# An encoder trunk of two layers: the latents' up-projection stacked on 128 rows, the first norm's rows kept in PSUM, and a newly ranked order of instructions

## The chip, the core and the metric

The kernel runs on one core of a Trainium2 chip. The metric is the device time of one execution in microseconds. Three runs of the kernel before took 1167.98, 1168.71 and 1168.90 us (median 1168.71).

## What is computed

The reference is a trunk of two post-norm layers over 512 positions of width 1024, in float32. Cut to what matters here:

```
h = layer_norm(x, ln_in_g, ln_in_b)
for l in range(2):
    a_in, b_q, b_k, b_v, c_in, d_cq, d_ckv, d_kr = split(h @ w_in[l])
    o_a = silu(layer_norm(depthwise_conv31(a_in[:256] * sigmoid(a_in[256:]))))
    o_b = attention(rope(rms_norm(b_q)), rope(rms_norm(b_k)), b_v)      # 4 heads of 64
    o_c = u * (sgu_w @ layer_norm(sv) + sgu_b)                          # u, sv = gelu(c_in)
    qd  = rms_norm(d_cq, mla_q_norm) @ mla_w_uq     # 192 latents -> 4 heads x 96
    kvd = rms_norm(d_ckv, mla_kv_norm) @ mla_w_ukv  # 128 latents -> 4 heads x 128
    o_d = attention(q, k, v from qd, kvd, rope(d_kr))                   # 4 heads of 96
    h = layer_norm(alpha * h + concat(o_a, o_b, o_c, o_d) @ w_out)
    f = conv3(h @ ffn_w_up); f = silu(f[:2816]) * f[2816:]
    h = layer_norm(alpha * h + f @ ffn_w_down)
```

## The kernel before

Positions lie in four tiles of 128. Every float32 operand of a matmul is split in a high part (rounded, made by ScalarE) and a low part (the rest, a subtraction on VectorE or GpSimd), and a product is three matmuls, high x high, high x low and low x high: `mm3` issues them. Weights come by DMA in chunks into three `raw` buffers and are split into `wh` and `wl` units on chip; the stream `h` is normalised by `ln_tile`, transposed on TensorE and split into `hh` and `hl`. PSUM has eight buffers, four called `acc` and four called `wk`.

The work of a layer is recorded as sections: the projections of the groups B (grouped-query attention), A (convolution), D (latents) and C (gating), normalisation and rotation, the up-projection of the latents (`d_up`), the attentions, the convolution's 31 steps on VectorE (`a_conv`), the output projection (`residual` with chunks O), the feed-forward part (`ffn`, chunks F) and its way down (`residual` with chunks W). In layer 0 group B comes first and A second.

The order on each engine isn't the order of recording. A planner (`Sched.place`) goes through the recorded operations with a table of costs and starts at each step the one that can begin first, by a priority: the operation's number plus the `rank` of its section. `window` and `slack` say how far ahead and how late an operation may be taken. Weight chunks have their own rule: `ahead` tells how many chunks before its use a chunk's DMA is issued, `lead` where the splitting stands. The resulting order is fixed in the program.

What the change touches: `first_rows` makes the scale and bias rows of the input's norm by transposing a column tile `incol` that is broadcast (16 transposes, four to a row of 512), each into a `wk` buffer that ScalarE copies to a unit called `row`. `LN_IN = "TTDS"` gives the four tiles' modes: T and D do the norm on VectorE (per half two instructions, `h = (h - mean) * g` and `h = h * r + b`), T at highest priority for the first half; S does it with ScalarE, VectorE and GpSimd. `rsqrt` computes r as a power on GpSimd (`vr <- ve, mhalf`). `d_evac` copies the 352 latent columns out of PSUM, `d_norm` scales them, `d_lat` transposes them (columns 0 to 127, 128 to 191 and 192 to 319) and splits them into `dTh` and `dTl`, and `d_up` multiplies: the 192 query latents are 128 rows and 64 rows, each a product of three matmuls, into the same buffer.

Of the kernel before, what the change touches and what calls it, by code (L numbers as in the profile page):

```python
# [16 lines left out]
P = 128  # L17
DM = 1024
S = 512
# [29 lines left out]
for _k in KEYS:  # L49
# [11 lines left out]
LN_IN, LN_MODES, LN_OUT = "TTDS", ["DDDD"] * 4, "DSST"  # L61
# [10 lines left out]
TUNE = {'window': 383,  # L72
         'slack': 11.0,
         'spare': 1,
         'ahead': {'A': 16, 'B': 21, 'D': 4, 'U': 18, 'V': 29, 'C': 42, 'O': 5, 'F': 6, 'W': 19},
         'lead': {'A': 19, 'B': 1, 'D': 33, 'U': 25, 'V': 3, 'C': 3, 'O': 0, 'F': 51, 'W': 13},
         'rank': {'a0': 141,
                  'a1': 91,
                  'a_norm1': -632,
                  'b1': -362,  # L80
                  'b_att0': 60,
                  'b_att1': 12,
                  'b_heads0': 234,
                  'b_heads1': -800,
                  'b_rope0': 56,
                  'b_rope1': -427,
                  'c0': -5,
                  'c1': -69,
                  'c_norm0': 147,
                  'c_norm1': -12,  # L90
                  'c_sgu0': -367,
                  'c_sgu1': -269,
                  'conv0': 481,
                  'conv1': -86,
                  'd0': 104,
                  'd_att0': -75,
                  'd_att1': -219,
                  'd_norm0': 294,
                  'd_norm1': -52,
                  'd_up0': -81,  # L100
                  'd_up1': 106,
                  'down0': -398,
                  'ffn0': -19,
                  'ffn1': 47,
                  'out0': 4,
                  'out1': -110,
                  'tables0': 1266,
                  'tables1': 123}}
# [98 lines left out]
class Op:  # L207
    __slots__ = ("eng", "cost", "tail", "lock", "calls", "deps", "succ", "nd", "prio", "ready", "allocs", "tiles", "spare",
                 "nbytes", "end", "start", "home", "sec", "after", "urgent", "table",
# [3 lines left out]
class Sched:  # L213
    ENGINES = ("SP", "PE", "DVE", "ACT", "POOL")

    def __init__(self, tc, pools):
# [3 lines left out]
        self.ops, self.group_op, self.sec, self.back, self.chunk_no = [], None, "", 0, None  # L220
# [31 lines left out]
    @contextmanager  # L252
    def chunk(self, j):

        old = self.chunk_no
        self.chunk_no = j
        yield
        self.chunk_no = old

    def record(self, eng, method, args, kw):  # L260
        op = self.group_op
        if not op:
# [4 lines left out]
            op.urgent, op.table = self.urgent, None  # L267
# [59 lines left out]
    def cost(eng, method, args, kw, outs, ins):  # L327
# [10 lines left out]
        if eng == "PE":  # L338
# [3 lines left out]
            if ins[0].shape[0] == 64 and n == 512 and psum(outs[0]) and outs[0].t.kind == "acc":  # L342
                return 115.0, 280.0, False
# [15 lines left out]
        if ALU.pow in args:  # L359
            return 290.0 + n * 165.0, 40.0, True  # L360
# [11 lines left out]
    def place(self, tune):  # L372

        extra = {}
        for op in self.ops:
            op.end, op.start, op.ready, op.spare, op.succ = 0.0, None, 0.0, 0, []
            op.nd = len(op.deps) + len(op.after)
            op.prio = -1 if op.urgent else op.index + tune["rank"].get(op.sec, 0)
            if op.chunk is not None:
                kind = KEYS[op.chunk][1]  # L380
                before = KEYS[max(0, op.chunk - tune["ahead"][kind])]
                op.home = self.first_use[before]
                if op.eng == "SP":
                    op.prio = op.chunk
                    if before in self.last_use and op.chunk >= tune["ahead"][kind]:
                        extra[op] = self.last_use[before]
                        op.nd += extra[op] not in op.deps
                else:
                    op.spare = tune["spare"]
                    op.prio = self.first_use[KEYS[max(0, op.chunk - tune["lead"][kind])]]  # L390
# [111 lines left out]
class Kern:  # L502
# [204 lines left out]
    def region(self, l, c, n, evac, single=False):  # L707
# [3 lines left out]
        for t in range(NT):  # L711
# [13 lines left out]
            evac(t, ps)  # L725
# [30 lines left out]
    def a_conv(self, l):  # L756
        s = self.s
        o = l * NPP
        for c in range(2):
# [171 lines left out]
    def b_heads(self):  # L931
        self.bq = [None] * 3
        for i in (2, 0, 1):
            ps = self.wk()
            self.transposes(ps, [y.rearrange("p h c -> p (h c)")[:, i * P:(i + 1) * P] for y in self.by])
            hi, lo = self.unit([P, S], FR, nm="bqh"), self.unit([P, S], FR, nm="bql")
            self.split(hi, lo, ps)
# [285 lines left out]
    def run(self):  # L1223
# [8 lines left out]
        for t in range(NT):  # L1232
            self.ln_tile(t, gb, LN_IN[t])
# [159 lines left out]
```

## Time and profile before

| | |
|---|---|
| median of three runs | 1168.71 us |
| the profiled execution | 1169.58 us, span 1167.8 us |
| TensorE (PE) busy | 1139.6 us, 98% |
| VectorE (DVE) busy | 778.6 us, 67% |
| ScalarE (ACT) busy | 559.7 us, 48% |
| GpSimd (POOL) busy | 162.2 us, 14% |
| mean granted clock of TensorE | 0.995 |

The span runs from the first to the last instruction. A busy share is a mean over stages that have different limits, so a stage's own windows and waits have to be read beside it. In a row of the timeline the first number is the start, the second the time from the first start to the last end of the merged instructions; in brackets stands the idle time of the engine before it, and what ended it. Matmuls overlap their neighbours, so the distance of two starts is what one costs, not its duration. The granted clock is given as a share of full speed: 1.00 is 2.4 GHz and 0.50 is 1.2 GHz.

### The profile page before, as it was taken

The numbers are of one execution on the slowest core, as the hardware profiler recorded it, in microseconds if no ns is written. First come the engines' busy times: TensorE is split into PE (matmuls) and PEld (weight loads), VectorE is DVE, ScalarE is ACT, GpSimd is POOL, SyncE is SP. The second block draws the span as 40 slices with busy tenths as digits, with TensorE's granted clock in tenths as the row PEclk, the third lists the DMA queues.
The fourth block names the chain that finished last, engine by engine and source line by source line (L and its number), as shares of the span: only waits on it lengthen the run. The fifth ranks groups of instructions, "written<-read, shape, count | busy, mean of one in ns | idle before, by whom it ended". The sixth has DMA issues, their size and how long they took to land.

```text
span 1167.8 us, 15419 instructions
## 1 busy us (share of the span) xinstructions
PE 1139.6 (98%) x5810; PEld 963.8 (83%) x5810; DVE 778.6 (67%) x1306; ACT 559.7 (48%) x1201; POOL 162.2 (14%) x205
## 2 busy tenths in 40 slices
PE   5999989999999999999999999999999999999997
PEld 4797878898888888888889888889888888888886
DVE  7798996876666755325586999967766676642425
ACT  4747897244444543223345579743544464431221
POOL 5325144100000000000022234230000000000002
PEclk9899999999999999999999999999999999999999
DMA  6520031233222522224432001222322353222311
GB/s 212 163 85 1 19 109 32 78 115 102 96 103 91 182 75 72 91 90 131 145 110 86 1 1 36 91 90 73 127 90 91 109 172 99 70 74 73 107 56 72
DMA packets 32041, 105.71 MB, mean 91 GB/s; under 512 B 3680, under 2 KB 4064, under 8 KB 31968
## 3 DMA queue, kind: packets, MB, share of 16 engines
q1 hardware_dynamic: 31968, 104.74, 27.6%
q8 instruction: 45, 0.74, 0.2%
q14 instruction: 28, 0.23, 0.1%
HBM read 102.63 MB, written 2.10 MB: 90 GB/s over the span
## 4 chain that ended last, share of the span: by engine, by line
PE 92%; ACT 4%; DVE 3%; issue 1%; DMA 1%; SPq 0%; DVEq 0%; ACTq 0%
PE acc L490 55%; PE wk L490 37%; ACT prob L490 1%; ACT pth L490 1%; DMA h<-in_x_dram 1%; DVE max L490 1%; DVE h L490 1%; DVE ptl L490 0%; ACT wh L490 0%; ACT c L490 0%; ACT dh L490 0%; ACT L490 0%; DVE mixl L490 0%; DVE aconv L490 0%; ACT do L490 0%
## 5 line engine op out<-in xcount | busy, mean ns | idle before, releaser
L490 DVE TENSOR_TENSOR wl<-raw,wh 128x512 fp32r<-128x512 f32 (+1 forms) x264 | 175.7, 700 | 94.9 <-ACT wh L490 51.7
L490 ACT ACTIVATE wh<-raw 128x512 fp32r<-128x512 f32 (+2 forms) x310 | 177.7, 614 | 55.9 <-DMA raw<-in_wst_dram 39.6
L490 PE MATMUL acc<-hh,wh 128*128 128x512 f32 (+1 forms) x544 | 191.7, 352 | 0.0
L490 PE MATMUL acc<-hh,wl 128*128 128x512 f32 (+1 forms) x544 | 191.3, 352 | 0.0
L490 PE MATMUL acc<-hl,wh 128*128 128x512 f32 (+1 forms) x544 | 191.3, 352 | 0.0
L490 PE MATMUL wk<-hh,wh 128*128 128x512 f32 x320 | 124.5, 389 | 0.0
L490 PE MATMUL wk<-hl,wh 128*128 128x512 f32 x320 | 124.5, 389 | 0.0
L490 PE MATMUL wk<-hh,wl 128*128 128x512 f32 x320 | 124.5, 389 | 0.0
L490 PEld LDWEIGHTS acc<-hl,wh 128*128 128x128 f32 x544 | 102.9, 189 | 13.7
L490 PEld LDWEIGHTS acc<-hh,wh 128*128 128x128 f32 x544 | 102.9, 189 | 13.7
L490 PEld LDWEIGHTS acc<-hh,wl 128*128 128x128 f32 x544 | 102.9, 189 | 13.7
L490 POOL TENSOR_TENSOR vr<-ve,mhalf 128x1 f32<-128x1 f32 (+2 forms) x26 | 26.6, 1021 | 593.0 <-DVE ve L490 592.9
L490 DVE SCALAR_TENSOR_TENSOR y<-acc,pp,y 128x511 f32<-128x511 f32 x96 | 71.9, 749 | 37.7 <-ACT y L490 35.8
L490 DVE TENSOR_TENSOR hl<-raw,hh 128x512 fp32r<-128x512 f32 x56 | 38.0, 690 | 83.5 <-ACT hh L490 83.5
L490 ACT ACTIVATE hh<-raw 128x512 fp32r<-128x512 f32 x56 | 35.4, 632 | 109.4 <-PE acc L490 92.0
L490 DVE SCALAR_TENSOR_TENSOR aconv<-aglu,pp,aconv 128x506 f32<-128x506 f32 (+14 forms) x120 | 86.8, 754 | 0.7
L490 PE MATMUL acc<-hl,fh 128*128 128x512 f32 x224 | 85.8, 383 | 0.0
L490 PE MATMUL acc<-hh,fh 128*128 128x512 f32 x224 | 85.7, 383 | 0.0
L490 PE MATMUL acc<-hh,fl 128*128 128x512 f32 x224 | 85.7, 382 | 0.0
L490 DVE SCALAR_TENSOR_TENSOR y<-wk,pp,y 128x511 f32<-128x511 f32 x80 | 60.0, 750 | 25.6 <-ACT y L490 23.8
L490 PE MATMUL wk<-wh,hh 128*128 128x512 f32 (+1 forms) x192 | 75.0, 391 | 0.7 <-DVE hl L490 0.7
L490 PE MATMUL wk<-wh,hl 128*128 128x512 f32 (+1 forms) x192 | 72.3, 376 | 0.0
(199 smaller groups left out, 2287.1 us busy)
## 6 DMA issues: line engine op xcount, KB each, us to landing
raw<-in_wst_dram SPq DMA_DIRECT2D x172, 512.0 KB, 3.5
row<-in_rows_dram SPq DMA_DIRECT2D x16, 256.0 KB, 4.8
raw<-in_wst_dram SPq DMA_DIRECT2D x8, 352.0 KB, 3.4
out_dram<-h SPq DMA_DIRECT2D x8, 256.0 KB, 2.0
h<-in_x_dram SPq DMA_DIRECT2D x3, 512.0 KB, 5.2
raw<-in_wst_dram SPq DMA_DIRECT2D x2, 384.0 KB, 4.0
h<-in_x_dram SPq DMA_DIRECT2D x2, 256.0 KB, 2.8
raw<-in_wst_dram SPq DMA_DIRECT2D x2, 256.0 KB, 2.8
```

What stands on the lines that cost most here:

```text
L490: f(*[a.real() if isinstance(a, View) else a for a in args], **{k: v.real() if isinstance(v, View) else v for k, v in kw.items()})
```

## The change

There are three edits.

The scale and bias rows of the first norm are transposed into `acc` buffers and stay there; VectorE reads them from PSUM, and the copies to `row` units are gone. The fourth input tile is normalised in mode D instead of S.

In the up-projection the second part of the query latents, 64 rows, is stacked: the 64 columns 128 to 191 are copied twice on evacuation (the latent unit grows from 352 to 416 columns), so that the transposed tile has the same 64 rows twice; the high part is made on all 128 rows and the lower 64 rows are then overwritten with the low part. The weight's 64 rows are laid out twice in the host's array, where zeros were before. One matmul with the weight's high part and one with its low part replace the three on 64 rows (the product low x low is computed as well).

The planner gets finer sections: a section can have parts (`with s.sub(...)`), whose rank is added to the section's, and `ahead` and `lead` can be given for a chunk kind in one layer. Three of its costs are changed, and the whole table of ranks, `ahead` and `lead` is replaced. What is recorded is otherwise the same.

```diff
-LN_IN, LN_MODES, LN_OUT = "TTDS", ["DDDD"] * 4, "DSST"
+LN_IN, LN_MODES, LN_OUT = "TTDD", ["DDDD"] * 4, "DSST"
...
-TUNE = {'window': 383,
-         'slack': 11.0,
+TUNE = {'window': 334,
+         'slack': 0.0,
...
+    @contextmanager
+    def sub(self, name):
+
+        old = self.part
+        self.part = f"{self.sec}.{name}"
+        yield
+        self.part = old
...
-                return 115.0, 280.0, False
+                return 115.0 + (200.0 if kw["start"] else 0.0) / 2 + (100.0 if kw["stop"] else 0.0) / 2, 280.0, False
...
-            return 290.0 + n * 165.0, 40.0, True
+            return 700.0 + n * 145.0, 40.0, True
...
-            op.prio = -1 if op.urgent else op.index + tune["rank"].get(op.sec, 0)
+            op.prio = -1 if op.urgent else op.index + tune["rank"].get(op.sec, 0) + tune["rank"].get(op.part, 0)
...
-                ps = self.wk()
+                ps = self.acc()
                 o = i * KD + 4 * j
                 self.transposes(ps, [self.incol[:, k:k + 1].to_broadcast([P, P]) for k in range(o, o + 4)])
-                u = self.unit([P, 512], nm="row")
-                self.s.ACT.activation(u, ps, AF.Copy)
-                res[i][j] = u
+                res[i][j] = ps
...
-            c = self.unit([P, 352], nm="dc")
+            c = self.unit([P, 416], nm="dc")
...
-            s.ACT.activation(c, ps[:, 0:352], AF.Copy)
+            s.ACT.activation(c[:, 0:192], ps[:, 0:192], AF.Copy)
+            s.ACT.activation(c[:, 192:416], ps[:, 128:352], AF.Copy)
...
-            s.ACT.activation(hi[:n], ps[:n], AF.Copy, scale=g)
-            s.DVE.scalar_tensor_tensor(lo_[:n], ps[:n], g, hi[:n].bitcast(F32), ALU.mult, ALU.subtract)
+            hi = self.unit([P, S], FR, nm="dTh")
+            g = self.pp[:, o + col:o + col + 1]
+            s.ACT.activation(hi, ps, AF.Copy, scale=g)
+            if n == P:
+                lo_, r = self.unit([P, S], FR, nm="dTl"), slice(0, P)
+            else:
+                lo_, r = hi, slice(n, P)
+            s.DVE.scalar_tensor_tensor(lo_[r], ps[r], g[r], hi[r].bitcast(F32), ALU.mult, ALU.subtract)
...
-                self.mm3(ps[:, 0:384], c1h[:64, ts], c1l[:64, ts], w1[0][:64], w1[1][:64], False, True)
+
+                s.PE.matmul(ps[:, 0:384], c1[:, ts], w1[0], start=False, stop=False)
+                s.PE.matmul(ps[:, 0:384], c1[:, ts], w1[1], start=False, stop=True)
...
-        pad = np.zeros((256, 384), uq.dtype)
-        pad[:192] = uq
-        wst.append(_ktiles(pad, 384))
+        wst.append(_ktiles(np.concatenate([uq, uq[128:]]), 384))
```

How the order moves is seen at three places. The first is VectorE at the program's start; `h_83` and `h_84` are the first and second input tiles, `mv` a tile's mean and variance, `vr` its r, and the rows are `row_...` before and `acc_...` after. Before:

```order
L490 TENSOR_SCALAR ve_119<-mv_112 128x1
L490 SCALAR_TENSOR_TENSOR h_83<-h_83,mv_112,row_121 128x512
L490 BN_STATS bst_144<-h_84 128x6 x2
L490 BN_AGGR mv_153<-bst_144 128x2
L490 SCALAR_TENSOR_TENSOR h_83<-h_83,vr_123,row_133 128x512
L490 TENSOR_SCALAR ve_163<-mv_153 128x1
L490 SCALAR_TENSOR_TENSOR h_84<-h_84,mv_153,row_121 128x512
L490 SCALAR_TENSOR_TENSOR h_83<-h_83,mv_112,row_146 128x512
L490 SCALAR_TENSOR_TENSOR h_84<-h_84,mv_153,row_146 128x512
L490 SCALAR_TENSOR_TENSOR h_83<-h_83,vr_123,row_150 128x512
```

On VectorE at the same place after the change:

```order
L610 TENSOR_SCALAR ve_119<-mv_112 128x1
L610 SCALAR_TENSOR_TENSOR h_83<-h_83,mv_112,acc_107 128x512
L610 SCALAR_TENSOR_TENSOR h_83<-h_83,vr_122,acc_114 128x512
L610 SCALAR_TENSOR_TENSOR h_83<-h_83,mv_112,acc_126 128x512
L610 BN_STATS bst_149<-h_84 128x6
L610 SCALAR_TENSOR_TENSOR h_83<-h_83,vr_122,acc_136 128x512
L610 BN_STATS bst_149<-h_84 128x6
L610 TENSOR_TENSOR hl<-wk_144,hh 128x4x128
L610 BN_AGGR mv_170<-bst_149 128x2
L610 SCALAR_TENSOR_TENSOR h_84<-h_84,mv_170,acc_126 128x512
```

All four multiplies of the first tile now stand ahead of the second tile's first multiply, with one statistics instruction between them where two and an aggregation stood.

The second place is GpSimd at the start, with the low parts `wl` of the first weight chunks and the powers `vr` of the input tiles. Before:

```order
L490 TENSOR_TENSOR wl_135<-raw_97,wh_125 128x512
L490 TENSOR_TENSOR wl_148<-raw_97,wh_137 128x512
L490 TENSOR_TENSOR vr_185<-ve_163,mhalf 128x1
L490 TENSOR_TENSOR wl_194<-raw_100,wh_155 128x512
L490 TENSOR_TENSOR wl_208<-raw_100,wh_160 128x512
L490 TENSOR_TENSOR wl_228<-raw_102,wh_172 128x512
```

On GpSimd at the same place after:

```order
L610 TENSOR_TENSOR wl_134<-raw_97,wh_124 128x512
L610 TENSOR_TENSOR wl_142<-raw_97,wh_131 128x512
L610 TENSOR_TENSOR wl_168<-raw_100,wh_161 128x512
L610 TENSOR_TENSOR wl_188<-raw_100,wh_165 128x512
L610 TENSOR_TENSOR wl_197<-raw_102,wh_184 128x512
L610 TENSOR_TENSOR vr_209<-ve_193,mhalf 128x1
L610 TENSOR_TENSOR wl_213<-raw_102,wh_190 128x512
```

The power of the second input tile moved behind three more low parts.

The third place is TensorE in the up-projection of layer 0, one position tile and the start of what follows. Before:

```order
L490 MATMUL wk_1084<-wh_375,dTh_1043 128x384
L490 MATMUL wk_1084<-wl_415,dTh_1043 128x384
L490 MATMUL wk_1084<-wh_375,dTl_1056 128x384
L490 MATMUL wk_1084<-wh_379,dTh_1047 128x384
L490 MATMUL wk_1084<-wl_425,dTh_1047 128x384
L490 MATMUL wk_1084<-wh_379,dTl_1062 128x384
L490 MATMUL wk_1096<-wh_375,dTh_1043 128x384
```

On TensorE at the same place after:

```order
L610 MATMUL wk_1167<-wh_476,dTh_1130 128x384
L610 MATMUL wk_1167<-wl_486,dTh_1130 128x384
L610 MATMUL wk_1167<-wh_476,dTl_1148 128x384
L610 MATMUL wk_1167<-wh_484,dTh_1138 128x384
L610 MATMUL wk_1167<-wl_498,dTh_1138 128x384
L610 MATMUL wk_1180<-wh_489,dTh_1150 128x512
L610 MATMUL wk_1180<-wl_507,dTh_1150 128x512
L610 MATMUL wk_1180<-wh_489,dTl_1161 128x512
```

The second part of the query latents (`dTh_1047` before, `dTh_1138` after) takes two matmuls instead of three, and the key and value part of the same position tile (the 512 columns) now follows at once instead of behind all query parts.

## Rows read from the trace of the kernel before

**Rows 1.** The page's first part: busy us, share of the span, instructions, by engine.

```profile
PE 1139.6 (98%) x5810; PEld 963.8 (83%) x5810; DVE 778.6 (67%) x1306; ACT 559.7 (48%) x1201; POOL 162.2 (14%) x205
```

**Rows 2.** Windows: stretch, length, busy us by engine (instructions), granted clock, DMA share, GB/s.

```profile
132.00:178.00 46.00, 42.08 (x264) 35.45 (x261) 44.06 (x86) 42.72 (x98) 14.18 (x12) 1.00 0.20 69
692.00:765.00 73.00, 69.54 (x428) 58.97 (x426) 63.99 (x127) 61.25 (x140) 27.38 (x27) 1.00 0.18 57
822.00:1030.00 208.00, 208.00 (x920) 172.27 (x919) 134.51 (x198) 96.61 (x158) 0.00 (x0) 1.00 0.33 107
1157.00:1168.00 11.00, 3.73 (x32) 3.52 (x30) 6.55 (x12) 0.81 (x2) 3.56 (x3) 0.82 0.25 95
```

**Rows 3.** Timeline of the start: start, us, engine, instruction, count, idle before and releaser.

```profile
5.12 3.65 PE L490 MATMUL wk<-ident,incol 128*128 128x128 f32 x16 [5.12 <-DMA incol<-in_incol_dram]
6.24 0.60 ACT L490 ACTIVATE row<-wk 128x512 f32<-128x512 f32 x1 [4.22 <-PE wk L490]
6.87 0.75 DVE L490 SCALAR_TENSOR_TENSOR h<-h,mv,row 128x512 f32<-128x512 f32 x1 [1.60 <-ACT row L490]
8.23 2.52 POOL L490 TENSOR_TENSOR wl<-raw,wh 128x512 fp32r<-128x512 f32 x2 [2.25 <-ACT wh L490]
9.03 1.29 DVE L490 BATCH_NORM_STATS2 bst<-h 128x6 f32<-128x512 f32 x2 [1.41 <-DMA h<-in_x_dram]
11.35 1.12 PE L490 MATMUL wk<-ident,h 128*128 128x128 f32 x4 [2.59 <-DVE ve L490]
11.44 0.99 POOL L490 TENSOR_TENSOR vr<-ve,mhalf 128x1 f32<-128x1 f32 x1 [0.69 <-DVE ve L490]
14.28 1.76 DVE L490 SCALAR_TENSOR_TENSOR h<-h,vr,row 128x512 f32<-128x512 f32 x1
16.09 1.12 PE L490 MATMUL wk<-ident,h 128*128 128x128 f32 x4 [3.62 <-DVE h L490]
16.86 0.78 PE L490 MATMUL wk<-wh,hh 128*128 128x512 f32 x1
17.43 0.63 PE L490 MATMUL wk<-wl,hh 128*128 128x512 f32 x1
17.86 0.63 PE L490 MATMUL wk<-wh,hl 128*128 128x512 f32 x1
29.62 1.37 PE L490 MATMUL wk<-ident,h 128*128 128x128 f32 x8 [1.67 <-issue]
```

**Rows 4.** Windows: the stretch behind the second wait.

```profile
31.60:37.00 5.40, 5.34 (x13) 4.18 (x14) 5.38 (x8) 3.63 (x7) 3.35 (x2) 0.50 0.51 174
```

**Rows 5.** The chain that ended last, in order of time: start, us, what.

```profile
31.66 17.65 PE wk L490 x68
49.31 10.88 PE acc L490 x48
```

**Rows 6.** Timeline of TensorE in the up-projections of layer 0 and of layer 1.

```profile
101.77 0.33 PE L490 MATMUL wk<-wh,dTl 128*128 128x384 f32 x1
102.03 0.44 PE L490 MATMUL wk<-wh,dTh 64*128 64x384 f32 x1
102.31 0.33 PE L490 MATMUL wk<-wl,dTh 64*128 64x384 f32 x1
102.49 0.33 PE L490 MATMUL wk<-wh,dTl 64*128 64x384 f32 x1
102.75 0.44 PE L490 MATMUL wk<-wh,dTh 128*128 128x384 f32 x1
...
690.75 0.44 PE L490 MATMUL wk<-wh,dTh 64*128 64x384 f32 x1
690.76 0.50 PE L490 MATMUL acc<-bqh,bqh 64*128 64x512 f32 x1
```

**Rows 7.** Groups of VectorE's instructions, shapes apart: busy us, mean ns, idle before.

```profile
L490 DVE SCALAR_TENSOR_TENSOR h<-h,mv,row 128x512 f32<-128x512 f32 x34 | 24.9, 773 | 1.6 <-ACT row L490 1.6
L490 DVE SCALAR_TENSOR_TENSOR h<-h,acc 128x512 f32<-128x512 f32 x31 | 21.3, 687 | 41.7 <-PE acc L490 41.7
```

More of the change, by code (lines that the diff above doesn't have):

```diff
@@ new lines @@
+         'ahead': {'A': 6,
+                   'B': 10,
+                   'D': 10,
+                   'U': 21,
+                   'V': 12,
+                   'C': 44,
+                   'O': 5,
+                   'F': 2,
+                   'W': 6,
+                   'W1': 35,
+                   'W0': 15,
+                   'C0': 42,
+                   'A1': 17,
+                   'V0': 17,
+                   'C1': 42,
+                   'F1': 6,
+                   'A0': 30,
+                   'B1': 34,
+                   'D0': 9,
+                   'F0': 5,
+                   'B0': 27,
+                   'V1': 28,
+                   'U1': 32,
+                   'U0': 40,
+                   'D1': 5},
@@ new lines @@
+         'lead': {'A': 32,
+                  'B': 14,
+                  'D': 45,
+                  'U': 73,
+                  'V': 8,
+                  'C': 0,
+                  'O': 5,
+                  'F': 37,
+                  'W': 8,
+                  'D1': 5,
+                  'A0': 11,
+                  'U1': 69,
+                  'C1': 11,
+                  'O1': 0,
+                  'D0': 22,
+                  'B1': 15,
+                  'F1': 16,
+                  'O0': 2,
+                  'U0': 84,
+                  'V1': 15,
+                  'V0': 15,
+                  'C0': 13,
+                  'B0': 3,
+                  'F0': 45,
+                  'A1': 30,
+                  'W0': 14,
+                  'W1': 6},
@@ L208 @@
     __slots__ = ("eng", "cost", "tail", "lock", "calls", "deps", "succ", "nd", "prio", "ready", "allocs", "tiles", "spare",
-                 "nbytes", "end", "start", "home", "sec", "after", "urgent", "table",
+                 "nbytes", "end", "start", "home", "sec", "after", "urgent", "table", "part",
                  "chunk", "index")
@@ L219, in __init__ @@
                         "POOL": tc.nc.gpsimd}
-        self.ops, self.group_op, self.sec, self.back, self.chunk_no = [], None, "", 0, None
+        self.ops, self.group_op, self.sec, self.part, self.back, self.chunk_no = [], None, "", "", 0, None
         self.group_wait, self.urgent = 0.0, False
@@ L377, in place @@
             op.nd = len(op.deps) + len(op.after)
-            op.prio = -1 if op.urgent else op.index + tune["rank"].get(op.sec, 0)
+            op.prio = -1 if op.urgent else op.index + tune["rank"].get(op.sec, 0) + tune["rank"].get(op.part, 0)
             if op.chunk is not None:
                 kind = KEYS[op.chunk][1]
-                before = KEYS[max(0, op.chunk - tune["ahead"][kind])]
+                layer = f"{kind}{KEYS[op.chunk][0]}"
+                ahead, lead = [tune[k].get(layer, tune[k][kind]) for k in ("ahead", "lead")]
+                before = KEYS[max(0, op.chunk - ahead)]
                 op.home = self.first_use[before]
@@ L384, in place @@
                     op.prio = op.chunk
-                    if before in self.last_use and op.chunk >= tune["ahead"][kind]:
+                    if before in self.last_use and op.chunk >= ahead:
                         extra[op] = self.last_use[before]
@@ L724, in region @@
                     self.used(l, c, kc)
-            evac(t, ps)
+            with s.sub(t):
+                evac(t, ps)
     def col_mm(self, l, c, i, out, cols, last):
@@ L756, in a_conv, with a_conv_half @@
     def a_conv(self, l):
+        for c in range(2):
+            self.a_conv_half(l, c)
+    def a_conv_half(self, l, c):
         s = self.s
         o = l * NPP
-        for c in range(2):
+        with s.sub(c):
             a = self.aglu[c]
@@ L934, in b_heads @@
             ps = self.wk()
-            self.transposes(ps, [y.rearrange("p h c -> p (h c)")[:, i * P:(i + 1) * P] for y in self.by])
             hi, lo = self.unit([P, S], FR, nm="bqh"), self.unit([P, S], FR, nm="bql")
-            self.split(hi, lo, ps)
+            with self.s.sub(i):
+                self.transposes(ps, [y.rearrange("p h c -> p (h c)")[:, i * P:(i + 1) * P] for y in self.by])
+                self.split(hi, lo, ps)
             self.bq[i] = (hi, lo)
```

191 lines of the change are left out of this document (127 added, 64 removed).

## The prediction

> **What bounds the kernel now.** I read the page's first part first: TensorE is busy 98% of the span [rows 1], so the time is TensorE's instructions plus what it idles. Next come the windows by stage [rows 2]. In 822 to 1030 us (the second layer's feed-forward part) it is busy all 208 us; there only fewer instructions could help. In the stretches with attention, 132 to 178 and 692 to 765 us, it idles 46.00 - 42.08 = 3.9 and 73.00 - 69.54 = 3.5 us, 7.4 in all, and VectorE is busy 44.06 of the first 46: a second engine at its limit. At the end, 1157 to 1168, the last normalisation runs almost without TensorE. The rest of the idle time is at the start, so I then read the timeline there [rows 3]. TensorE's first instruction is at 5.12 us, its first matmul with a weight at 16.86 (the next ones at 17.43 and 17.86, a step of 0.43 us), and before 29.62 and 31.66 it waits again. Behind the second wait the granted clock is 0.50, that is 1.2 GHz [rows 4], after a stretch from 27.95 on in which it did nothing but eight transposes. The chain of waits in order of time gives a clean milestone [rows 5]: group A's first matmul at 49.31, with every one of group B's 96 matmuls and the 12 remaining transposes-by-four before it. In both orders exactly these stand ahead of it.
>
> The profiled execution took 1169.58 us, 1.8 more than its span and 0.9 above the median of the three runs; sums are made against 1169.58 and 0.9 is taken off at the end.
>
> **1. Rows of the first layer norm stay in PSUM; its fourth tile takes the same path as the others.** Before, ScalarE copied each of four rows out of PSUM (0.60 us), two of them behind weight copies, and VectorE's first multiply waited 1.60 us for that copy, starting at 6.87. Then two statistics instructions of the second input tile (1.29 us, waiting 1.41 for their DMA at 9.03) stood ahead of the next multiply, and the second half of tile 0 got its last multiply at 14.28, so its transposes started at 16.09.
> The new order, with these durations: the four rows are in PSUM a quarter of 3.65 us apart, at 6.0, 6.9, 7.9 and 8.8. Multiplies of 0.75 us: 6.2 to 7.0, 7.0 to 7.8, 8.0 to 8.8; one statistics instruction when its DMA is in, 9.03 to 9.7; the last multiply to 10.45. Transposes (1.12 for four): behind the rows' own, 8.8 to 9.9, and 10.5 to 11.6. The first weights' high and low parts are there (VectorE has no part in them; GpSimd makes the first two low parts from 8.23 to 10.75). First matmul at 11.6 instead of 16.86: 5.3 us.
> From there to group A: 96 matmuls at 10.88/48 = 0.227 us [rows 5] are 21.8. The first eight or so at 0.43 add 1.6, as they did before. Six groups of four transposes at about 0.5 are 3.0 (1.37 for eight at 29.62, some of it waiting). Waits that I find in the new order: the second tile's power on GpSimd stands behind three low parts of 1.26 us (10.8 to 15) and itself takes 0.99 [rows 3], so that tile's last multiplies end near 17 while TensorE is through the matmuls ahead of its transposes at 16: 1.2 us. The third and fourth tiles' multiplies end near 27 where TensorE comes at 25.2: 1.5. Their low parts stand behind weight subtractions: 0.6. Sum 21.8 + 1.6 + 3.0 + 3.3 = 29.7, so group A starts at 41.3 instead of 49.31. In the old stretch 13 matmuls at 1.2 GHz (2.6 us) and 2.4 us of waits stood there that have no counterpart. I take off half a microsecond for handoffs not counted: **-7.5**. Bounds: -10 if only 1.3 us of waits remain; -2.5 if two of the waits each bring the clock down for 13 matmuls as at 31.66 (2 x 13 x 0.2 = 5.2).
> A multiply that reads a row from PSUM is not in the trace; the nearest rows are 687 ns with one PSUM operand and 773 with all in SBUF [rows 7], and it is taken at the upper one's size. Of the fourth tile, two ScalarE passes and two GpSimd additions go and two VectorE instructions come: 1.5 us more on VectorE, inside the 1.5 us wait above. The Trainium skill speaks against this edit: "VectorE: DVE Perf Modes", Rules for kernel authors, advises copying a matmul's output to SBUF first when many operations read it, and here four rows are each read four times. By that rule, with a surcharge of a tenth of the upper row's 773 ns for each read (an estimate), 16 x 0.08 = 1.2 us would come to VectorE and at most that much to the sum. The two rows show no surcharge for PSUM.
>
> **2. The up-projection's 64-row part.** Before, each of 8 position tiles has three matmuls on 128 rows and three on 64; after, three and two, all on 128. The timeline of the first layer [rows 6] shows what a 64-row part costs. In a run the starts are 0.18 us apart (102.31 to 102.49), but across a change of row count 0.26 (101.77 to 102.03, 102.49 to 102.75), and the step after it 0.28 (102.03 to 102.31): 0.09 + 0.10 for each change. A tile thus saves 0.18 + 2 x 0.19 = 0.56; eight make 4.5. Counted in the order, changes between 64 and 128 rows fall from 30 to 13, which with eight matmuls is 8 x 0.18 + 17 x 0.19 = 4.7. One thing comes off: in the second layer a 64-row part stands next to the score matmuls of the other 64 rows, and they start 0.01 us apart (690.75, 690.76): there it was nearly free, some 0.4 us. I take **-4.2**; bounds -1.4 (the matmuls alone) and -4.7. The Trainium skill has that case as a rule: "TensorEngine Tiling (Array Packing)", Overview, says that contractions of at most 64 rows can share the array for up to twice the speed. By it alone nothing would be gained where partners stand beside them, and term 2 would be 0.7 us smaller for each tile so placed; in the first layer's rows all three sit on the same 64 rows in sequence, so the rows decide for the sum.
> What the edit adds hangs on ScalarE: the latents' evacuation becomes two copies instead of one (eight more instructions, each at most half of the 0.60 us that a copy of 512 columns takes in [rows 3]) and a slightly longer scaling. ScalarE is busy 42.72 of 46 us in the first attention stretch; I cost it at nothing because these evacuations stand ahead of that stretch and TensorE waits for none of them now; uncovered it would be 8 x 0.3 = 2.4.
>
> **3. The other order (sections ranked in finer parts).** In the two feed-forward parts TensorE's order is the same over long runs and the last instructions of every engine are the same, so there I expect nothing. In the attention stretches two counts change. In the first layer VectorE gets 10 more instructions between the first and the last maximum: 13 more convolution steps of about 0.75 us, the length of the multiply in [rows 3], less three others, some 7 us. But TensorE gets 46 more between the same scores (466 before, 512 after), which at the 0.227 us of a 512-column matmul and less for narrower ones is some 8 us, so the load of the one against the other does not grow. In the second layer VectorE has seven instructions fewer and TensorE six more. And places where a PSUM buffer is rewritten with under 1.3 us of TensorE work in between fall from 13 to 5. So the 7.4 us of idling should shrink, to about 5: **-2.5**; bounds -6 (nearly all goes) and +5 (VectorE's 7 us more come to lie uncovered, less 2 saved in the second layer).
>
> Sum: -7.5 - 4.2 - 2.5 = -14.2. 1169.58 - 14.2 = 1155.4, less 0.9: **1154.5 us**.
>
> **Rivals.**
> - *The start gives most of it back.* The new order has three short waits before group A, where the old has a long one. If they bring the granted clock to 0.50 as at 31.66, or GpSimd's low parts (each 1.26 us, the eighth near 20 us) hold TensorE longer, term 1 is -2.5 to -4 and the time 1158 to 1160. For it: the old trace's clock fell after a broken wait. Against: TensorE had waited twice there within a short stretch, 1.67 us and, before 31.66, another 0.7; the waits that I find are shorter. Further, late inputs (a DMA a few us later than before) would bring it to 1160 to 1165.
> - *VectorE becomes the bound in attention (the other side).* It is at 44.06 of 46 us, and the first layer's stretch gets 13 more convolution steps, 13 x 0.75 = 9.8 us. If TensorE's 8 us of added work are not beside them, TensorE idles up to 9.8 more there; with the same in the second layer, where three score-to-transposes distances shrink from over 4 to about 3 us of TensorE work, the idling goes from 7.4 to 23 or more. From about 19 us on, the gains of terms 1 and 2 are gone and the kernel is slower: 1171 to 1175. Against: the counts of term 3, where TensorE's work grows with VectorE's.
> - *The edit to the up-projection does nothing for TensorE*, because what follows waits for ScalarE's evacuations (in the new order both up-projections of a tile alternate, eight evacuations in a row). Then term 2 is +0.5 instead of -4.2 and the time 1159.
>
> **How the numbers follow.** Forecast 0.60 (its own range 1150 to 1158); the start gives back, or inputs come late 0.19; up-projection hidden 0.08; VectorE binds 0.07; a mixture that ends near the old time 0.06. The range runs over the first two rivals: 1147 (both upper bounds in part) to 1164. The measurement tells 0.2%, 2.3 us, from no change: faster 0.88, same 0.05, slower 0.07.
>
> **What would show it.** Term 1: group A's first matmul near 41 us; the first weight matmul near 11.6; a granted clock of 0.50 behind 16 or 25 us would be the rival. Term 2: starts 0.18 us apart through a tile's five matmuls. Term 3: TensorE's waits for "ptl", "bo", "dl", "prob" summing to about 5 us. The forecast is wrong if group A starts after 46 us, or if the idling in attention exceeds 12.

## The result and the profile after

The changed kernel takes **1155.24 us** (median of 4 runs, 1154.78 to 1156.6) against 1168.74 (4 runs, 1167.98 to 1168.9): ratio 0.9888, 95% interval 0.9871 to 0.9905, faster by 13.5 us. The forecast was 1154.5, from 1147 to 1164. The profiled execution took 1155.01 us, its span is 1153.2: 14.6 less than before in both.

The page's first part [rows 1]:

```profile
PE 1131.9 (98%) x5802; PEld 959.7 (83%) x5802; DVE 771.0 (67%) x1307; ACT 558.2 (48%) x1203; POOL 169.4 (15%) x203
```

Windows by stage [rows 2], moved 10 to 15 us forward with the stages (the first is 50 us long where it was 46):

```profile
120.00:170.00 50.00, 47.56 (x299) 40.70 (x299) 48.26 (x94) 41.38 (x97) 15.59 (x13) 1.00 0.19 64
680.00:753.00 73.00, 70.51 (x440) 59.90 (x439) 62.50 (x126) 63.04 (x143) 21.72 (x21) 1.00 0.16 50
812.00:1020.00 208.00, 208.00 (x920) 172.22 (x919) 133.35 (x196) 96.72 (x157) 0.00 (x0) 1.00 0.32 105
1142.00:1153.00 11.00, 4.15 (x35) 3.95 (x33) 6.92 (x12) 1.23 (x2) 3.55 (x3) 0.90 0.25 95
```

TensorE idles 2.4 and 2.5 us in the attention stretches, where it idled 3.9 and 3.5; the feed-forward part and the end are as they were. The start [rows 3]:

```profile
4.71 3.25 PE L610 MATMUL acc<-ident,incol 128*128 128x128 f32 x16 [4.71 <-DMA incol<-in_incol_dram]
5.83 0.75 DVE L610 SCALAR_TENSOR_TENSOR h<-h,mv,acc 128x512 f32<-128x512 f32 x1 [0.29 <-PE acc L610]
10.37 3.82 POOL L610 TENSOR_TENSOR wl<-raw,wh 128x512 fp32r<-128x512 f32 x3 [0.41 <-ACT wh L610]
14.15 0.56 POOL L610 TENSOR_TENSOR vr<-ve,mhalf 128x1 f32<-128x1 f32 x1
14.80 0.69 DVE L610 BATCH_NORM_STATS2 bst<-h 128x6 f32<-128x512 f32 x1 [1.63 <-DMA h<-in_x_dram]
15.41 1.39 DVE L610 SCALAR_TENSOR_TENSOR h<-h,vr,acc 128x512 f32<-128x512 f32 x2
```

The first multiply no longer waits for a copy. The first matmul with a weight is at 10.23 us, where it was at 16.86; the next wait ends at 16.20, after 2.47 us for the second tile's multiplies. These multiplies stand behind a statistics instruction that waits for the third tile's DMA until 14.80. The clock behind that wait [rows 4] and the chain [rows 5]:

```profile
16.00:21.00 5.00, 4.80 (x19) 3.95 (x20) 4.15 (x10) 1.20 (x2) 4.06 (x5) 0.67 0.83 323
21.00:25.00 4.00, 4.00 (x19) 3.31 (x18) 3.94 (x10) 3.81 (x17) 2.30 (x4) 0.99 0.42 173
```

```profile
16.20 23.62 PE wk L610 x108
39.82 5.44 PE acc L610 x24
```

In the first of these windows the clock was at 1.2 GHz for a part: the matmuls from 19.71 to 20.99 start 0.42 to 0.43 us apart, then the clock was full and the step 0.23. Group A starts at 39.82 instead of 49.31. An up-projection [rows 6], and the next matmul behind it:

```profile
95.04 0.33 PE L610 MATMUL wk<-wh,dTh 128*128 128x384 f32 x1
95.22 0.34 PE L610 MATMUL wk<-wl,dTh 128*128 128x384 f32 x1
95.39 0.34 PE L610 MATMUL wk<-wh,dTl 128*128 128x384 f32 x1
95.57 0.35 PE L610 MATMUL wk<-wh,dTh 128*128 128x384 f32 x1
95.75 0.34 PE L610 MATMUL wk<-wl,dTh 128*128 128x384 f32 x1
95.93 0.40 PE L610 MATMUL wk<-wh,dTh 128*128 128x512 f32 x1
```

Five starts 0.17 to 0.18 us apart: 0.89 us a tile, where it was 1.43 (101.32 to 102.75). VectorE's first multiplies by form [rows 7], and TensorE's waits over the whole span without the first one, 4.7 us for `incol` (total, times, longest):

```profile
L610 DVE SCALAR_TENSOR_TENSOR h<-h,mv,acc 128x512 f32<-128x512 f32 x8 | 5.7, 737 | 0.4 <-PE acc L610 0.3
L610 DVE SCALAR_TENSOR_TENSOR h<-h,vr,acc 128x512 f32<-128x512 f32 x8 | 5.6, 739 | 0.2 <-PE acc L610 0.2
```

```profile
PE wk L610 <- DVE h L610: 3.9, 2, 2.5
PE wk L610 <- DVE ptl L610: 1.9, 3, 1.2
PE acc L610 <- ACT prob L610: 1.9, 5, 0.5
PE wk L610 <- DVE bo L610: 1.1, 1, 1.1
```

**Ledger of the 14.6 us**, by TensorE's starts: group A begins 9.49 earlier; from there to the last matmul 1111.1 became 1106.0, which is 2.1 less of waits (7.0 to 4.9), 4.0 less in the up-projections (16.7 to 12.7), and 1.0 more in the rest (transposes +1.7, others -0.7).

### The profile page after: what moved, and what is told of

Read it like the earlier page. It is cut to its first block, busy times and chain, and to the rows that moved or that the text cites. A ratio compares the mean times of both kernels' runs of the same rounds, so it can differ in the third digit from the quotient of the medians.

```text
span 1153.2 us, 15412 instructions
## 1 busy us (share of the span) xinstructions
PE 1131.9 (98%) x5802; PEld 959.7 (83%) x5802; DVE 771.0 (67%) x1307; ACT 558.2 (48%) x1203; POOL 169.4 (15%) x203
## 4 chain that ended last, share of the span: by engine, by line
PE 90%; ACT 5%; DVE 2%; DMA 1%; issue 1%; POOL 0%; SPq 0%; DVEq 0%; ACTq 0%
PE acc L610 55%; PE wk L610 35%; ACT prob L610 2%; ACT pth L610 1%; ACT wh L610 1%; DVE ptl L610 1%; ACT c L610 1%; DVE aconv L610 0%; DMA raw<-in_wst_dram 0%; DMA h<-in_x_dram 0%; ACT do L610 0%; DVE max L610 0%; DVE bo L610 0%; ACT mixh L610 0%; ACT bo L610 0%
## 5 line engine op out<-in xcount | busy, mean ns | idle before, releaser
L610 DVE TENSOR_TENSOR wl<-raw,wh 128x512 fp32r<-128x512 f32 (+1 forms) x264 | 171.6, 688 | 85.6 <-ACT wh L610 60.6
L610 DVE SCALAR_TENSOR_TENSOR aconv<-aglu,pp,aconv 128x501 f32<-128x501 f32 (+14 forms) x120 | 86.7, 758 | 0.6
L610 POOL TENSOR_TENSOR wl<-raw,wh 128x512 fp32r<-128x512 f32 (+1 forms) x46 | 59.8, 1320 | 91.6 <-ACT wh L610 58.3
```

What stands on the lines that cost most here:

```text
L610: f(*[a.real() if isinstance(a, View) else a for a in args], **{k: v.real() if isinstance(v, View) else v for k, v in kw.items()})
```

## The experiments

Every kernel was timed beside the kernel before (1167.4 to 1168.2 us there), and its ratio is to that time. The first matmul of the span, which hangs on a DMA, began at 4.27 to 5.78 us in these profiles; where the start is judged, "run-up" is group A's start less that moment: 44.2 before, **35.1** in the changed kernel.

**1 and 2. The up-projection, order held.** The last two matmuls of a tile become three, on the upper 64 rows (e1) or on all 128 (e2). The third repeats the product with the weight's high part, so e1 leaves out the low part of these latents and e2 adds one product twice.

```diff
+        for op, ps, c1, ts, w1 in self.up_ops:
...
+            mm = [(o, c1[:64, ts], w[:64]) for w in (w1[0], w1[1], w1[0])]   # e1
...
+            mm = [(o, c1[:, ts], w) for w in (w1[0], w1[1], w1[0])]         # e2
...
```

> The changed kernel with its order held; only the up-projection's second part issues three matmuls on the upper 64 rows again instead of two on 128 (the third repeats the high part, so the low part of those latents is left out). Theory (a change of row count costs two slow steps): each of eight tiles takes 0.18 + 2 x 0.19 = 0.56 us longer, 4.5 in all; in the timeline the five starts 0.18 apart become six, with steps of 0.26 to 0.28 at both changes; total about 1159.5. Rival 1 (only the columns count): 8 x 0.18 = 1.4, about 1156.7. Rival 2 (TensorE is held by ScalarE's evacuations there): within 0.5 us of the changed kernel, 1155.5.

> The changed kernel with its order held; the up-projection's second part issues three matmuls, all on 128 rows (the first product is added twice). Theory: one more step of 0.18 us in each of eight tiles and no change of row count, 1.4 us, total about 1156.7; the distance to the kernel with three on 64 rows is the price of the changes, 8 x 0.38 = 3.0. Rival 1 (only the columns count): the same time as that kernel. Rival 2 (ScalarE's evacuations hold TensorE): 1155.5.

Measured: 1158.51 (ratio 0.9919, 0.9904 to 0.9934) and 1156.21 (0.9900, 0.9886 to 0.9915). Summed over all up-projections, the start distances grew by 4.40 and 1.39 us against the changed kernel. The tile with 64 rows:

```profile
95.35 0.34 PE L610 MATMUL wk<-wh,dTl 128*128 128x384 f32 x1
95.61 0.44 PE L610 MATMUL wk<-wh,dTh 64*128 64x384 f32 x1
95.89 0.34 PE L610 MATMUL wk<-wl,dTh 64*128 64x384 f32 x1
```

The steps of 0.26 and 0.28 are back as soon as the row count changes. Of the 4.4 us, 1.4 is a third matmul in each of eight tiles and 3.0 the change of row count alone: shown. The time lost is less: from group A to the last matmul it took 3.3 and 0.8 us longer than in the changed kernel, because the waits there were 0.6 shorter in both, and in e1 the other matmuls and transposes 0.5.

**3 and 4. What holds the second tile.** The third tile's DMA goes ahead of the fourth weight chunk's; or the second tile's power goes ahead of two of GpSimd's low parts and the statistics behind that tile's multiplies.

```diff
+        move(x2, d, 0)                                # x2_swap
...
+        move(find("ve_13"), find("mv_12"), 1)         # pow_early
+        move(find("vr_14"), find("wl_43"), 0)
+        move(first, max(mults, key=self.order.index), 1)
```

> The changed kernel with its order held but for one DMA: the third input tile's load stands ahead of the fourth weight chunk's, so it no longer waits for a raw buffer (issue at 9.99 us now). Theory (the wait of 2.47 us before 16.20 hangs on that DMA, because the third tile's statistics stand ahead of the second tile's last multiplies on VectorE): those statistics start by 13.5 instead of 14.80, the multiplies when the power is there at 14.7, TensorE's transposes at about 15.5; group A starts 0.7 earlier, and 1.4 more if the seven matmuls at half rate behind it go: total 1153 to 1154.5. Rival (the power on GpSimd ends that wait): no change, 1155.2.

> The changed kernel with its order held but for three instructions: the second input tile's power stands behind one of GpSimd's three low parts instead of all three, what it needs from VectorE is moved up with it, and the third tile's statistics stand behind the second tile's last multiplies. Theory (power and statistics together hold these multiplies until 15.4): multiplies from 13.1, transposes at about 13.9 where TensorE comes at 13.7; the wait of 2.47 us falls under 0.5 and the half rate behind it goes; GpSimd's later low parts come 0.56 us later and may cost up to 1 us: group A starts 1.5 to 3.5 earlier, total 1152 to 1154. Rival (the low parts on GpSimd, 1.26 us each, bound this stretch anyway): group A within 0.5 us of 39.8, total 1155.

Measured: 1154.2 (0.9885, 0.9871 to 0.9900), run-up 33.8; and 1154.78 (0.9888, 0.9871 to 0.9904), run-up 34.1. The wait behind the first matmuls, and the clock after it, with the DMA moved:

```profile
14.79 1.41 DVE L610 SCALAR_TENSOR_TENSOR h<-h,vr,acc 128x512 f32<-128x512 f32 x2 [0.65 <-POOL vr L610]
15.60 0.65 PE L610 MATMUL wk<-ident,h 128*128 128x128 f32 x4 [1.65 <-DVE h L610]
```

```profile
16.00:21.00 5.00, 5.00 (x27) 4.04 (x26) 4.72 (x11) 1.94 (x4) 4.80 (x7) 1.00 1.00 375
```

So the late DMA ended that wait in the changed kernel, and GpSimd's power stands right behind it; in this profile no half rate followed. This time was as forecast. The other's forecast, 1152 to 1154, was missed, and the rival's time came: the power moved that early hands the wait to the low parts (1.2 us in three waits). In their profiles both gain about 1 us at the start; their times can't be told from the changed kernel's.

**5 to 8. Which edit carries the gain?** The old kernel with the rows edit alone, the up-projection's alone, both; and the changed kernel's planner and table without either. Each order is planned anew by the planner it has.

```diff
...
-                u = self.unit([P, 512], nm="row")                # rows_only, both_old_plan
-                self.s.ACT.activation(u, ps, AF.Copy)
-                res[i][j] = u
+                res[i][j] = ps
...
+                s.PE.matmul(ps[:, 0:384], c1[:, ts], w1[0], start=False, stop=False)   # up_only, both_old_plan
+                s.PE.matmul(ps[:, 0:384], c1[:, ts], w1[1], start=False, stop=True)
...
```

> The kernel before with one of the three edits: the four rows of the first layer norm stay in PSUM and all four input tiles take VectorE's path; the old planner and its old table then make the order. On VectorE the first multiplies, statistics and low parts come out as in the changed kernel up to the second tile (only that tile's two multiplies and a low part are in another order). Theory (the edit itself frees the start): group A's first matmul at 39 to 41.5 instead of 49.3, so 8 to 10 us less there. Behind it the order differs from before in some 225 of TensorE's rows without having been ranked for it; by the theory's third term (idling in attention 7 us before, 5 in the changed kernel) that may cost 0 to 4. Time 1158 to 1163. Rival (the start's gain is the ranked order's, the edit without it gives little): group A at 45 or later, time 1164 to 1169.

> The kernel before with the up-projection's edit alone (hi and lo of the latents stacked on 128 rows), old planner and table. Theory: TensorE's work between group A's first matmul and the last matmul falls by 4.0 (as the start distances of the up-projections' matmuls did in the changed kernel), group A stays at 49.3, time 1164.7 plus 0 to 3 for an order that was not ranked for it. Rival (the re-ranked order was needed for the up-projection's gain, since ScalarE's eight further evacuations delay attention): attention's waits, 7 before, go above 10 and the time is 1168 or more.

> The changed kernel without its two edits to the arithmetic's form: rows copied to SBUF, the fourth tile on ScalarE and GpSimd, the up-projection with 128 and 64 rows; only the finer sections, the planner's costs and the new table stay. Theory (the order is worth about 1 to 2.5): group A at 47 to 50, since the first multiply still waits for ScalarE's copy, attention's waits 5 to 8; time 1166 to 1169. Rival (the order carries most of the gain): below 1160, with group A below 44. A third way: the table was ranked for other instructions, and without them attention's waits exceed 10: 1170 or more.

> Both edits, old planner and old table: what the finer ranking adds is the changed kernel's time less this one's. Theory: start and up-projection add, 1168.7 - 9 - 4 = 1155.7, plus 0 to 4 for an order that was not ranked for it: 1156 to 1160, group A at 39 to 41.5, TensorE's work from there to the last matmul 4 less than before, attention's waits 7 to 11. Rival (VectorE binds in attention unless the sections are ranked anew): waits above 14, time above 1162.

Measured, with the intervals of the ratio, and from the profiles the change against before in us (start: group A; waits, up-projections and other work: from there to the last matmul):

| kernel | us | ratio | start | waits | up-proj. | other work |
|---|---|---|---|---|---|---|
| rows alone | 1166.50 | 0.9992 (0.9982-1.0001) | -7.7 | +3.1 | 0.0 | +2.1 |
| up-projection alone | 1171.27 | 1.0034 (1.0022-1.0046) | -2.3 | +4.8 | -3.2 | +2.2 |
| both, old table | 1165.79 | 0.9985 (0.9976-0.9995) | -5.7 | +3.4 | -3.0 | +3.2 |
| order alone | 1228.85 | 1.0529 (1.0512-1.0547) | | | | |
| changed kernel | 1155.24 | 0.9888 (0.9871-0.9905) | -9.5 | -2.1 | -4.0 | +1.0 |

The order alone mixes the groups, so it has no such milestone. The profile before took 1169.58, 2.2 more than its median beside the first four kernels (1167.37); so a row's sum lies some 2 us below what the times say for the rows alone (-2.5 and -0.9) and the up-projection alone (+1.5 and +3.9).

All four times that the theory gave were too low. The rivals' times held, their mechanisms only in part: with the rows alone group A is at 41.6, not 45; with the up-projection alone waits are 11.8 (above 10, as it said), but the longest are for VectorE, none for ScalarE's new copies; with both they are 10.3, not 14. For the order alone the third way held. The edits do what they should also under the old table (first weight matmul at 10.76 with the rows alone; up-projections 3 us shorter), but what they save is given back further on. In the kernel with the rows alone a wait in the attention grew from 1.51 to 1.95 us, and behind it the clock falls, which stayed at 1.00 before. The wait before, with the rows alone, and the clock there:

```profile
151.05 0.64 PE L490 MATMUL wk<-ident,dq 128*96 128x128 f32 x4 [1.51 <-DVE bo L490]
146.21 0.64 PE L490 MATMUL wk<-ident,dq 128*96 128x128 f32 x4 [1.95 <-DVE bo L490]
```

```profile
145.00:153.00 8.00, 6.71 (x34) 5.65 (x35) 6.95 (x13) 7.87 (x19) 6.02 (x5) 0.79 0.55 158
```

The old table was ranked for the old instructions; with others it sets an order that nobody ranked. The new table alone shows it at its worst: 61 us more. Behind its first weight matmul TensorE waits 48 us, where it waited 9.3, in many waits of at most 7.6, and the mean granted clock is 0.982 instead of 0.995; its longest waits in sum:

```profile
PE wk L610 <- DVE bz L610: 7.6, 1, 7.6
PE wk L610 <- DVE ptl L610: 7.6, 12, 0.9
PE acc L610 <- ACT prob L610: 7.2, 11, 1.3
PE acc L610 <- ACT mixh L610: 6.2, 2, 3.7
```

Ranking anew is thus worth some 11 us (ratio 0.9985 to 0.9888) once both edits are in, and the edits give 13.5 only together with it. Two things were not tested: which part of the new planner does it (the finer sections, the three costs or the table), and what a table ranked anew for the old instructions would have given. So the share of the 13.5 us that the edits alone would bring, each side at its best order, stays open.

**9 and 10. The rows' place, order held.** ScalarE copies the rows to SBUF; the multiplies read the copies (copy_rows), or the copies are made and not read (copy_only).

```diff
...
+                op.eng, op.calls, op.allocs = "ACT", [("activation", (u, ps, AF.Copy), {})], [u]
+                self.order.insert(self.order.index(made) + 1, op)
...
+                        o.calls = [(m, tuple(u if a is ps else a for a in args), kw) for m, args, kw in o.calls]   # copy_rows
```

> The changed kernel with its order held on every engine, but ScalarE copies the four rows from PSUM to SBUF (each copy right behind its row's transposes) and VectorE's multiplies of the first layer norm read the copies. Theory (two prices of SBUF rows: the copy itself, and VectorE and GpSimd holding each other up when a multiply has both its tensor operands in SBUF beside GpSimd's low parts, since in the kernel before such multiplies took up to 1.76 us and GpSimd's five low parts 1.55 each instead of 1.26): the first multiply waits about 1 us more, so the first weight matmul is at 11.5 to 12.5 instead of 10.2 to 10.8; multiplies beside GpSimd take 1.0 to 1.8 us instead of 0.70 to 0.75, those behind the second tile's power end 1 to 2 us later, and group A starts 1.5 to 3.5 us later, at 41 to 43.5. Time 1156.8 to 1159. Rival (the order of the statistics and multiplies alone makes the start, the place of the rows is indifferent): multiplies 0.75 us, group A within 0.7 us of 39.8, time 1154.8 to 1156. Second rival (by copying PSUM first, multiplies get cheaper): under 1155.

> As the previous kernel, the same four copies on ScalarE, but nobody reads them: the multiplies read PSUM as in the changed kernel. It prices the copies alone. Theory: the copies (4 x 0.60 us) stand ahead of the weights' high parts on ScalarE, GpSimd's low parts start about 1.5 us later and the first high part of the input too; multiplies keep 0.70 to 0.75 us. Group A 0 to 1.2 us later than 39.8, time 1155 to 1156.5; what the previous kernel loses beyond this is the operands' place. Rival (the copies are the whole price): as late as the previous kernel.

Measured: 1158.93 (0.9921, 0.9906 to 0.9936), run-up 38.6; and 1155.8 (0.9895, 0.9880 to 0.9909), run-up 36.0. Both times are as the theory said. VectorE's multiplies with SBUF rows, GpSimd's low parts beside them, and the second tile's transposes:

```profile
7.53 0.75 DVE L610 SCALAR_TENSOR_TENSOR h<-h,mv,row 128x512 f32<-128x512 f32 x1 [2.45 <-ACT row L610]
8.95 7.73 POOL L610 TENSOR_TENSOR wl<-raw,wh 128x512 fp32r<-128x512 f32 x5 [3.15 <-ACT wh L610]
9.39 1.50 DVE L610 SCALAR_TENSOR_TENSOR h<-h,mv,row 128x512 f32<-128x512 f32 x1 [0.19 <-ACT row L610]
13.93 3.31 DVE L610 SCALAR_TENSOR_TENSOR h<-h,mv,row 128x512 f32<-128x512 f32 x2
18.49 4.71 POOL L610 TENSOR_TENSOR wl<-raw,wh 128x512 fp32r<-128x512 f32 x3
18.56 3.47 DVE L610 SCALAR_TENSOR_TENSOR h<-h,vr,row 128x512 f32<-128x512 f32 x2
20.38 0.66 PE L610 MATMUL wk<-ident,h 128*128 128x128 f32 x4 [1.71 <-DVE h L610]
```

The same from the copies that nobody reads:

```profile
6.90 0.75 DVE L610 SCALAR_TENSOR_TENSOR h<-h,mv,acc 128x512 f32<-128x512 f32 x1 [1.74 <-ACT row L610]
8.32 6.47 POOL L610 TENSOR_TENSOR wl<-raw,wh 128x512 fp32r<-128x512 f32 x5 [2.44 <-ACT wh L610]
12.11 1.41 DVE L610 SCALAR_TENSOR_TENSOR h<-h,mv,acc 128x512 f32<-128x512 f32 x2
17.14 1.12 PE L610 MATMUL wk<-ident,h 128*128 128x128 f32 x4 [2.56 <-DVE h L610]
```

Where GpSimd is idle (7.53) a multiply with SBUF rows takes 0.75; beside a low part it takes 1.17 to 1.78, and the low parts take 1.55 each instead of 1.29. With a PSUM operand neither is touched. Of the rows' 3.5 us of run-up, 0.9 is the copies and 2.6 the operands' place: the first multiply waits for ScalarE's copy in both (1.75 us behind TensorE's first matmul, 1.12 in the changed kernel), so that wait is in the 0.9. The 2.6 are there at the second tile's transposes, which wait for VectorE in both: 20.38 - 5.78 = 14.60 us behind the first matmul against 17.14 - 5.15 = 11.99; from there to group A both take 24.0. TensorE's clock differs between the two, at 1.2 GHz up to 18.24 in copy_rows and behind 17.14 in copy_only. The Trainium skill has this as a rule: "SBUF — State Buffer", Who interferes with whom: an instruction of VectorE with two SBUF inputs contends with one of GpSimd that reads SBUF; one with at most one SBUF input, outside VectorE's 2-port modes, does not. The trace agrees, on both sides (up to 1.78 against 0.75 us on VectorE, 1.55 against 1.29 on GpSimd).

**11 and 12. A better start.** First, besides an earlier power and later statistics of the third tile, the sixth low part moves to VectorE and two bias additions move back; then only the earlier power (behind four low parts) with the third tile's DMA ahead.

```diff
...
+        o.eng, o.calls = "DVE", [("tensor_sub", a[:3], {})]   # tuned
+        move(o, stt[7], 1)
...
+        move(ve[1], mv[1], 1)                                 # x2_pow
+        move(vr[1], wl[3], 1)
+        move(xs[3], ch[3], 0)
```

> The changed kernel with seven instructions of the start moved, the order else held: the second tile's variance and power earlier (the power behind four low parts instead of five), the third tile's first statistics behind the second tile's last multiplies, one low part (the sixth) from GpSimd to VectorE, and two bias additions behind the fourth tile's last multiplies. Theory: TensorE's waits between its first weight matmul and group A fall from 2.5 us (and seven matmuls at half rate, 1.4 us) to about 0.5 to 1, so group A starts at 38 to 38.7 instead of 39.8, time 1153 to 1154. Rival (GpSimd's low parts or the third weight chunk's DMA hold TensorE instead): waits of 1.5 us or more by other names, group A at 39.2 or later, time 1154.5 to 1155.5.

> The changed kernel with three of the start's instructions moved: the third input tile's DMA ahead of the fourth weight chunk's, the second tile's variance ahead of its first multiplies, its power on GpSimd behind four low parts instead of five. All eight low parts stay on GpSimd, so no instruction of VectorE with both operands in SBUF stands beside GpSimd's, as the moved low part did that took 1.70 us. Theory: the wait of 1.65 us before the second tile's transposes (with the DMA moved alone) falls to about 0.5, low parts add waits of up to 0.3 twice, group A at 38.2 to 39.1, no half rate before it, time 1153 to 1154.2. Rival (the moved DMA makes the fourth chunk's low parts late): waits for low parts above 1 us, group A at 39.5 or later, time 1154.5 to 1155.5.

Measured: 1154.85 (0.9886, 0.9869 to 0.9902), run-up 35.7: the rival's time, though by another cause. The moved low part has both its inputs in SBUF and stands beside GpSimd's:

```profile
13.74 4.25 POOL L610 TENSOR_TENSOR wl<-raw,wh 128x512 fp32r<-128x512 f32 x3
15.14 1.70 DVE L610 TENSOR_TENSOR wl<-raw,wh 128x512 fp32r<-128x512 f32 x1
16.90 0.50 PE L610 MATMUL wk<-wl,hh 128*128 128x512 f32 x1 [0.69 <-DVE wl L610]
```

1.70 us instead of 0.68, and TensorE waits for it; another wait of 0.99, behind the moved additions, stands before 28.72. The last kernel: 1154.39 (0.9886, 0.9869 to 0.9902), just above its forecast; group A at 38.60 as forecast, but only because its first DMA came early: run-up 34.3, no better than with the DMA moved alone (33.8). Its first wait fell from 1.65 to 0.85, and a later one, at 23.70, grew from 0.61 to 0.94. No version is shown to beat the changed kernel.

## Why the prediction was right, and where its steps were off

- **Term 1, forecast -7.5, measured -9.5.** Right in kind. From the first weight matmul to group A it took 29.6 us, forecast 29.7, but by other parts: waits 2.5 instead of 3.3 (one, by the third tile's DMA, instead of three), half rate about 1.4 instead of 1.6 and at another place, transposes with their handoffs 3.9 instead of 3.0. The first weight matmul came at 10.23 instead of 11.6: 0.4 of it by an earlier DMA in that run, and 0.7 because the granted clock was 1.00 from 7.42 us on, so that the four transposes ahead of it took 0.41 and not 1.1 (9.82 to 10.23). The half microsecond taken off at the end was not needed. The wait of 1.5 us for the third and fourth tiles didn't come.
- **What the forecast missed in term 1** is why the old start was late. It named the copy and the statistics. The row at 14.28 [rows 3], a multiply of 1.76 us, stood there unexplained: the eight multiplies of the first two tiles took 9.2 us (0.75, 0.82, 3.07 for three, 1.76, 1.18, 1.61) instead of 8 x 0.74, and GpSimd's power 0.99 instead of 0.56. Each long one (the last of the three and the three behind it) stands beside a low part. Experiments 9 and 10 show what that costs in the changed kernel's order: 2.6 us, and 3.5 with the copies, of the 9.1 by which the run-up fell. What it cost in the old order was not measured by itself. The rule weighed in the prediction, copying PSUM to SBUF before many reads, makes it worse here: 737 and 739 ns with a PSUM row, no surcharge, and up to 1.78 us with an SBUF row.
- **Term 2, forecast -4.2, measured -4.0** (undone: +4.4 in the matmuls' starts, 3.3 from group A to the last matmul). The price of a change of row count, 0.09 + 0.10, held, and so, about, did the 0.4 taken off for 64-row parts that stand beside others (eight tiles at 1.43 - 0.89 would be 4.3). The count behind the upper bound does not hold: over the span, in order of starts, changes between 64 and 128 rows fall from 38 to 28, not from 30 to 13. ScalarE's extra copies cost TensorE no wait here, so the third rival did not come.
- **Term 3, forecast -2.5, measured -2.1 of waits and +1.0 of work.** The waits fell to 4.9, forecast about 5. The step that failed is the idea that the order is a small term beside two edits: alone it is +61, and the edits without it give 1.6 of 13.5. The order in the changed kernel was read as it stands; its terms can't be had singly. The added work lies in transposes, of `prob` (+1.0) and `recs` (+0.8). Standing next to 64-row matmuls explains little of it: nine transposes are followed by one instead of six, at 0.20 us each in both, some 0.3 in all. The cause stays open.
- **The sum.** Forecast -14.2, measured -14.6 in the profiles. That they lie so close is in part luck: term 1 gave 2.0 more than forecast, and term 3 with the added work 1.4 less.
- **Rivals.** That the start gives most back: a half-rate stretch behind 16 us came, as named, and cost 1.4, not 4. VectorE binding in attention didn't come in the ranked order. With the old table waits of 10 to 12 us did, short of the 19 it needed; with the new table alone there were 48, for VectorE and ScalarE both.

## What to carry to other kernels

A table that ranks instructions fits one set of instructions only: judge an edit either with the order held word for word, or ranked anew on both sides; an edit tried under the old ranking can look worthless or harmful while its mechanism works. Here the order was held in the experiments on single edits; ranking anew on both sides was not tried. When an instruction takes twice its group's usual time, ask what runs beside it before pricing its removal. For VectorE next to GpSimd, leaving an operand in PSUM was worth more (2.6 us) than the copies it saved (0.9).

## What was not expected of the hardware

- VectorE and GpSimd held each other up where both read two operands of 512 columns from SBUF: 0.75 became 1.2 to 1.8 us, and 1.29 became 1.55.
- A wait can cost twice, and its length alone doesn't tell when. Behind waits of 1.95 and 2.40 us (rows alone), 2.47 (changed kernel), 2.56 (copy_only), 2.83 (both, old table) and also 1.80 (e1) the granted clock showed 0.58 to 0.79 of full in the following stretch, that is 1.2 GHz in part of it. Behind 1.65 (DMA moved), 1.71 (copy_rows) and 1.88 (up-projection alone, at 694.25) it stayed at 1.00. What decides stays open.
- A window of the profile can print a full clock where the steps say otherwise. In copy_rows the windows before 18 us show 1.00, but that trace has no record of the clock before 18.3, and matmuls of 512 columns start 0.43 us apart there, the step at 1.2 GHz:

```profile
13.98 0.63 PE L610 MATMUL wk<-wl,hh 128*128 128x512 f32 x1
14.40 0.63 PE L610 MATMUL wk<-wh,hl 128*128 128x512 f32 x1
14.83 0.63 PE L610 MATMUL wk<-wh,hh 128*128 128x512 f32 x1
```

- The DMA of `incol`, 8 KB, let TensorE start anywhere from 4.27 to 5.78 us; a difference of 1 us in one profile's milestones says nothing until that is taken off.
